# The gating products of four tokens in one turn of the generator, in a kernel of two transformer blocks

## The chip, the cores and the metric

The kernel runs on one core of one Trainium2 chip. The time is the device time of one execution in microseconds (us); lower is better. The engines of the core are TensorE (PE in the profile, its weight loads PEld), VectorE (DVE), ScalarE (ACT), GpSimd (POOL) and SyncE (SP), which here issues DMAs. Each runs its own instructions in order and waits for others by semaphores.

## The reference, cut to what matters

Two blocks are computed, one after the other, on 256 tokens of width 1024. The part that is changed lies in the first block, in a layer of experts that each head picks for each token. Of 16384 experts, numbered (i, j) with i and j from 0 to 127, each of 8 heads picks 16 per token and gives each a gate.

```python
def expert_block(args):
    ht, it, gt = args
    ue = jnp.take(u, it, axis=0)
    act = jax.nn.gelu(jnp.einsum('tkd,td->tk', ue, ht), approximate=False)
    ve = jnp.take(v, it, axis=0)
    return jnp.einsum('tk,tkd->td', gt * act, ve)
```

The kernel takes no rows out of u or v. It multiplies all of u with all tokens, applies the Gelu, and multiplies by a dense matrix of gates that is zero for experts not picked; then it multiplies all of v with the result.

## The kernel before, in words

The weights come in pieces of 128 x 1024, one piece for a slot. A piece is loaded by SyncE's queue (wraw, four buffers), cast by ScalarE to a high part (wh) and subtracted by VectorE to a low part (wl), and each product is made of three matmuls: hH with wh, hL with wh, hH with wl. In the part of u a slot makes one row j of 128 experts for all 256 tokens: 24 matmuls into a PSUM tile named v, 12 in each half of the slot. ScalarE then applies the Gelu and VectorE multiplies by the gates where they are known already. The rows are kept in bigA (72 rows) and bigB (56 rows).

The gates of a token are a 128 x 128 matrix, made on TensorE as a product of two one-hot matrices over the token's 128 picks: A (ohA) has the place of j, B (ohB) the place of i times the gate. `onehots(g)` makes those of a pair of tokens (NG is 2): VectorE makes A of both and B of the first; B of the second is made on ScalarE in two steps (Abs, then Relu) or on VectorE, as a model of the engines' clocks decides when the program is built. There are three buffers of such pairs. `gates_mm(g, pg)` multiplies a pair into half of a PSUM tile pg for four tokens, which is named mm or aux in turn. `gates_ev(g, pg)` takes four tokens out of PSUM: for rows that are made already (there are J of them) VectorE multiplies the gates into bigA and bigB; for the rows still to come ScalarE copies the gates there, and the row is multiplied when it is made (`ev_u`).

`g_gates` is a generator that does all of this between the u products. `slot` and `half` call `step()`, once after the first half of the products and once after the second, and each `step()` advances every generator by one turn, as long as the modelled clocks of VectorE and ScalarE aren't too far ahead of TensorE's. The cast wh for the slot after the next but one is issued behind the first `step()` of a slot, the subtraction wl for the next but one ahead of its second. The order that comes out is fixed when the program is built. All engine calls go through one helper, so the profile gives them line 217; they are told apart by their tiles.

At the start of the gating 44 rows of u are made, so 84 slots of u follow.

Of the kernel before, what the change touches and what calls it, by code (L numbers as in the profile page):

```python
# [22 lines left out]
F32 = mybir.dt.float32  # L23
# [8 lines left out]
T = 256  # L32
# [275 lines left out]
def build(tc, xT, memT, smalls, smalls2, w1, keysT, uT, vT, w2, outT, stop=None):  # L308
# [8 lines left out]
    ps = es.enter_context(tc.tile_pool(name="ps", bufs=2, space=PSUM))  # L317
# [919 lines left out]
    NK = NKEY  # L1237
# [65 lines left out]
    NG = 2  # L1303
# [147 lines left out]
    def onehots(g):  # L1451
        t = NG * g
        A, B = ohs[g % 3]
        V.tensor_tensor(A, iota[:, None, :].to_broadcast([128, NG, 128]),
                        idxT[0][:, t:t + NG, None].to_broadcast([128, NG, 128]), op=OP.is_equal)
        for q in range(NG):
            i2, gg = idxT[1][:, t + q:t + q + 1], idxT[2][:, t + q:t + q + 1]
            if q % 2 and clock.t["S"] < clock.t["V"] + 500:

                S.activation(B[:, q], iota, AF.Abs, scale=-1.0, bias=i2)  # L1460
                S.activation(B[:, q], B[:, q], AF.Relu, scale=ngT[:, t // 2:t // 2 + 1], bias=gg)
            else:
                V.tensor_scalar(B[:, q], iota, i2, gg, op0=OP.is_equal, op1=OP.mult)
        oh[g] = (A, B)

    def gates_mm(g, pg):
        A, B = oh.pop(g)
        for q in range(NG):
            PE.matmul(pg[:, g % 2 * NG + q], A[:, q], B[:, q], start=True, stop=True)

    def gates_ev(g, pg):
        J = st["j"]
        ts = slice(4 * g, 4 * g + 4)
        for b, j0, j1 in bigs:
            lo, hi = j0, min(j1, J)
            if hi > lo:
                view = b[:, lo - j0:hi - j0, ts].rearrange("p j t -> p t j")
                V.tensor_tensor(view, view, pg[:, :, lo:hi], op=OP.mult)
            lo = max(j0, J)
            if j1 > lo:  # L1480
                view = b[:, lo - j0:j1 - j0, ts].rearrange("p j t -> p t j")
                S.copy(view, pg[:, :, lo:j1])
        st["g"] = g + 1

    def g_gates():
        onehots(0)
        onehots(1)
        yield
        pend = None
        for k in range(T // NG):  # L1490
            if k % 2 == 0:
                pg = ps.tile([128, 4, NK], F32, name="mm" if k % 4 else "aux")
            gates_mm(k, pg)
            if k % 2 == 0 and pend is not None:
                gates_ev(*pend)
            if k + 2 < T // NG:
                onehots(k + 2)
            pend = (k // 2, pg)
            clock.at(0.0)
            yield  # L1500
        gates_ev(*pend)

    go(g_gates())
    lim[0] = 2 * LIMIT
    while nu < NK:
# [26 lines left out]
    k = 0  # L1532
# [876 lines left out]
```

## Time and profile before

| what | value |
| --- | --- |
| time, median of 3 runs | 1461.38 us (1456.76 to 1477.7) |
| the profiled execution's own time | 1469.8 us |
| its span, first to last instruction | 1468.1 us |
| TensorE busy, mean granted clock | 97% of the span, 0.991 |
| VectorE, ScalarE, GpSimd busy | 73%, 58%, 12% |
| the gating | from the first one-hot at 388.5 us to the last at 622.8 us |
| u slots without gating behind it | until 684 us |

Busy shares are those of the whole span. The stages differ much from this mean, so they are read by windows of their own. A matmul's duration in the trace is longer than the step from its start to the next one's, since matmuls overlap; the same holds, less so, for short instructions on ScalarE and VectorE.

### The profile page before, as it was taken

The page shows a single profiled execution, that of the slowest core. Times are in us where ns is not written, and L with a number is a line of the kernel's source. Part 1 is how long each engine was busy: PE and PEld are TensorE (multiplying, and loading weights), DVE is VectorE, ACT ScalarE, POOL GpSimd, SP SyncE. Part 2 cuts the span into 40 slices and gives each one's busy share as a digit, 9 for nine tenths or more (in the row PEclk, how much of TensorE's full clock was granted, in tenths as well). Part 3 has the DMA queues.
Part 4 walks back from the last instruction along what each step waited for, and adds up shares of the span by engine and source line. Part 5 has one row for each costly group of instructions (what it writes and reads, how often), then busy time and mean ns, then how long its engine had stood idle before and what let it go on. Part 6 is the DMA issues. An engine that isn't in the chain of part 4 may idle for free.

```text
span 1468.1 us, 30208 instructions
## 1 busy us (share of the span) xinstructions
PE 1426.5 (97%) x11904; PEld 1398.6 (95%) x11904; DVE 1075.8 (73%) x2096; ACT 850.1 (58%) x1617; POOL 181.2 (12%) x228
## 2 busy tenths in 40 slices
PE   8999999999999999999999999999999999999997
PEld 8799998999999999999999989999998899999996
DVE  7866679899888999955555557555699774786665
ACT  5753454445699998844444455454575554655553
POOL 6100032014300000000000030000025420410000
PEclk9999999999999999999999999999999999999998
DMA  6334553545544443454555565555532443455552
GB/s 216 130 115 144 174 200 132 198 162 176 172 143 144 143 143 144 145 186 173 186 185 187 202 219 190 199 188 200 171 127 80 159 170 114 172 189 188 186 187 72
DMA packets 66381, 242.64 MB, mean 165 GB/s; under 512 B 7488, under 2 KB 7488, under 8 KB 65856
## 3 DMA queue, kind: packets, MB, share of 16 engines
q1 hardware_dynamic: 65664, 237.01, 47.0%
q0 software_dynamic: 432, 3.69, 0.7%
q8 instruction: 93, 1.52, 0.4%
q14 instruction: 48, 0.39, 0.1%
q10 hardware_dynamic: 144, 0.03, 0.0%
HBM read 239.64 MB, written 1.05 MB: 164 GB/s over the span
## 4 chain that ended last, share of the span: by engine, by line
PE 83%; DVE 9%; POOL 3%; issue 2%; ACT 2%; DMA 1%; DVEq 0%; ACTq 0%; POOLq 0%
PE v L217 49%; PE mm L217 28%; PE aux L217 6%; DVE wl L217 2%; DVE yc L217 1%; DMA s2t<-smalls_dram 1%; DVE x L217 1%; POOL hL L217 1%; DVE eq L217 1%; DVE hL L217 0%; POOL eq L217 0%; DVE pos L217 0%; DVE nt L217 0%; DVE xa L217 0%; ACT wh L217 0%
## 5 line engine op out<-in xcount | busy, mean ns | idle before, releaser
L217 DVE TENSOR_TENSOR wl<-wraw,wh 128x1024 fp32r<-128x1024 f32 x444 | 556.0, 1255 | 56.9 <-issue 45.7
L217 ACT CAST wh<-wraw 128x1024 fp32r<-128x1024 f32 x444 | 463.9, 1045 | 227.4 <-issue 123.5
L217 PE MATMUL v<-hH,wh 128*128 128x256 f32 x2048 | 583.5, 285 | 1.4 <-ACT hH L217 1.4
L217 PE MATMUL v<-hH,wl 128*128 128x256 f32 x2048 | 571.6, 279 | 4.3 <-DVE wl L217 4.3
L217 PE MATMUL v<-hL,wh 128*128 128x256 f32 x2048 | 571.5, 279 | 2.1 <-POOL hL L217 2.0
L217 PEld LDWEIGHTS v<-hH,wl 128*128 128x128 f32 x2048 | 386.7, 189 | 6.3 <-DVE wl L217 6.3
L217 PEld LDWEIGHTS v<-hL,wh 128*128 128x128 f32 x2048 | 386.7, 189 | 3.3 <-POOL hL L217 3.1
L217 PEld LDWEIGHTS v<-hH,wh 128*128 128x128 f32 x2048 | 385.4, 188 | 1.9 <-ACT hH L217 1.9
L217 PE MATMUL mm<-hH,wh 128*128 128x256 f32 x656 | 190.7, 292 | 7.7 <-DVE au L217 3.9
L217 PE MATMUL mm<-hL,wh 128*128 128x256 f32 x656 | 184.0, 284 | 3.1 <-DVE hL L217 2.5
L217 PE MATMUL mm<-hH,wl 128*128 128x256 f32 x656 | 185.5, 284 | 1.1 <-DVE wl L217 1.1
L217 PEld LDWEIGHTS mm<-hH,wh 128*128 128x128 f32 x656 | 127.1, 194 | 12.5 <-ACT wh L217 4.7
L217 PEld LDWEIGHTS mm<-hL,wh 128*128 128x128 f32 x656 | 125.7, 193 | 4.2 <-DVE hL L217 3.1
L217 PEld LDWEIGHTS mm<-hH,wl 128*128 128x128 f32 x656 | 126.8, 193 | 1.7 <-DVE wl L217 1.6
L217 DVE TENSOR_TENSOR hL<-bigA,hH 128x256 fp32r<-128x256 f32 x72 | 31.7, 441 | 77.5 <-ACT hH L217 77.4
L217 PE MATMUL mm<-h5H,wh 128*128 128x256 f32 x272 | 76.4, 281 | 0.0
L217 PE MATMUL mm<-h5L,wh 128*128 128x256 f32 x272 | 76.4, 281 | 0.0
L217 PE MATMUL mm<-h5H,wl 128*128 128x256 f32 x272 | 76.4, 281 | 0.0
L217 DVE TENSOR_TENSOR hL<-bigB,hH 128x256 fp32r<-128x256 f32 x56 | 23.8, 426 | 68.3 <-ACT hH L217 68.3
L217 ACT ACTIVATE ohB<-ohB,gT,ngT 128x128 f32<-128x128 f32 x126 | 62.3, 494 | 4.2
L217 ACT ACTIVATE bigA<-v 128x256 f32<-128x256 f32 (+14 forms) x72 | 25.8, 358 | 67.1 <-PE v L217 67.1
L217 DVE TENSOR_TENSOR ohA<-iota,i1T 128x256 f32<-128x256 f32 x128 | 53.6, 419 | 13.5 <-PE aux L217 6.5
(548 smaller groups left out, 2402.6 us busy)
## 6 DMA issues: line engine op xcount, KB each, us to landing
wraw<-w_dram SPq DMA_DIRECT2D x192, 512.0 KB, 3.5
wraw<-uT_dram SPq DMA_DIRECT2D x128, 512.0 KB, 3.3
wraw<-vT_dram SPq DMA_DIRECT2D x128, 512.0 KB, 3.3
s2t<-smalls_dram POOLq DMA_DIRECT2D x1, 1552.0 KB, 13.4
x<-xT_dram SPq DMA_DIRECT2D x4, 256.0 KB, 5.6
kyT<-keysT_dram POOLq DMA_DIRECT2D x1, 1024.0 KB, 7.1
xm<-memT_dram POOLq DMA_DIRECT2D x1, 1024.0 KB, 8.8
outT_dram<-z SPq DMA_DIRECT2D x4, 256.0 KB, 2.8
```

Source lines behind the costliest of these rows:

```text
L217: r = f(out, *a, **k)
```

## The change

`g_gates` makes the one-hots of three pairs at its start instead of two, and in each turn it now multiplies two pairs (four tokens, one PSUM tile), takes the four tokens of the turn before out of PSUM, and makes the one-hots of the next two pairs. Before, a turn had one pair, and every second turn took four tokens out.

```diff
     def g_gates():
-        onehots(0)
-        onehots(1)
+        for g in range(3):
+            onehots(g)
         yield
         pend = None
-        for k in range(T // NG):
-            if k % 2 == 0:
-                pg = ps.tile([128, 4, NK], F32, name="mm" if k % 4 else "aux")
+        for k in range(0, T // NG, 2):
+            pg = ps.tile([128, 4, NK], F32, name="mm" if k % 4 else "aux")
             gates_mm(k, pg)
-            if k % 2 == 0 and pend is not None:
+            gates_mm(k + 1, pg)
+            if pend is not None:
                 gates_ev(*pend)
-            if k + 2 < T // NG:
-                onehots(k + 2)
+            for g in (k + 3, k + 4):
+                if g < T // NG:
+                    onehots(g)
             pend = (k // 2, pg)
             clock.at(0.0)
             yield
         gates_ev(*pend)
```

On TensorE, at the first gating products, before (the numbers behind ohA and ohB are those of the buffers):

```order
L217 MATMUL v<-hH,wl 128x256
L217 MATMUL aux<-ohB_4839,ohA_4838 128x128 x2
L217 MATMUL v<-hH,wh 128x256
L217 MATMUL v<-hL,wh 128x256
L217 MATMUL v<-hH,wl 128x256
```

And now, at the same place:

```order
L217 MATMUL v<-hH,wl 128x256
L217 MATMUL aux<-ohB_4839,ohA_4838 128x128 x2
L217 MATMUL aux<-ohB_4841,ohA_4840 128x128 x2
L217 MATMUL v<-hH,wh 128x256
L217 MATMUL v<-hL,wh 128x256
L217 MATMUL v<-hH,wl 128x256
```

Two pairs stand together. In both kernels 12 products into v lie between one such block and the next, all through the gating: there are 128 blocks of one pair before and 64 of two pairs now, so the last one comes after 32 slots instead of 64.

On ScalarE, one slot in the middle of the gating, before:

```order
L217 COPY bigA<-aux 128x4x14
L217 COPY bigB<-aux 128x4x56
L217 ACTIVATE ohB_4843<-iota,i2T 128x128
L217 ACTIVATE ohB_4843<-ohB_4843,gT,ngT 128x128
L217 ACTIVATE bigA<-v 128x196
L217 ACTIVATE v<-v 128x60
L217 ACTIVATE ohB_4839<-iota,i2T 128x128
L217 ACTIVATE ohB_4839<-ohB_4839,gT,ngT 128x128
L217 CAST wh<-wraw 128x1024
```

And now, from the cast of one slot to shortly before the next cast:

```order
L217 CAST wh<-wraw 128x1024
L217 COPY bigA<-mm 128x4x18
L217 COPY bigB<-mm 128x4x56
L217 ACTIVATE ohB_4843<-iota,i2T 128x128
L217 ACTIVATE ohB_4843<-ohB_4843,gT,ngT 128x128
L217 ACTIVATE ohB_4839<-iota,i2T 128x128
L217 ACTIVATE ohB_4839<-ohB_4839,gT,ngT 128x128
L217 ACTIVATE bigA<-v 128x168
L217 ACTIVATE v<-v 128x88
L217 COPY bigA<-aux 128x4x17
L217 COPY bigB<-aux 128x4x56
```

Behind these come two more one-hots, of two steps each, and then the next cast. A slot has two pairs of copies and four one-hots where it had one and two; the cast and the two Gelus stay single.

On VectorE, one slot in the middle of the gating, before:

```order
L217 TENSOR_TENSOR bigA<-bigA,aux 128x4x58
L217 TENSOR_TENSOR ohA_4842<-iota,i1T 128x256
L217 TENSOR_SCALAR ohB_4843<-iota,i2T,gT 128x128
L217 TENSOR_TENSOR bigA<-bigA,v 128x56
L217 TENSOR_TENSOR ohA_4838<-iota,i1T 128x256
L217 TENSOR_SCALAR ohB_4839<-iota,i2T,gT 128x128
L217 TENSOR_TENSOR wl<-wraw,wh 128x1024
```

And now:

```order
L217 TENSOR_TENSOR bigA<-bigA,v 128x56
L217 TENSOR_TENSOR bigA<-bigA,aux 128x4x52
L217 TENSOR_TENSOR ohA_4840<-iota,i1T 128x256
L217 TENSOR_SCALAR ohB_4841<-iota,i2T,gT 128x128
L217 TENSOR_TENSOR ohA_4842<-iota,i1T 128x256
L217 TENSOR_SCALAR ohB_4843<-iota,i2T,gT 128x128
L217 TENSOR_TENSOR wl<-wraw,wh 128x1024
L217 TENSOR_TENSOR bigA<-bigA,mm 128x4x52
L217 TENSOR_TENSOR ohA_4838<-iota,i1T 128x256
L217 TENSOR_SCALAR ohB_4839<-iota,i2T,gT 128x128
L217 TENSOR_TENSOR ohA_4840<-iota,i1T 128x256
L217 TENSOR_SCALAR ohB_4841<-iota,i2T,gT 128x128
```

The multiplies of the gates and the one-hots are doubled for each wl. In all, 126 one-hots B are made on ScalarE and 130 on VectorE in both kernels. Behind the gating the rows of every engine stand in the same order as before, up to the numbers of buffers.

## Rows read from the trace of the kernel before

**Rows 1.** The page's first part: busy us, share of the span, instructions.

```profile
PE 1426.5 (97%) x11904; PEld 1398.6 (95%) x11904; DVE 1075.8 (73%) x2096; ACT 850.1 (58%) x1617; POOL 181.2 (12%) x228
```

**Rows 2.** Windows: us, busy of PE, PEld, DVE, ACT, POOL; granted clock, DMA share, GB/s.

```profile
390.00:508.00 118.00, 118.00 (x1027) 118.00 (x1026) 103.48 (x226) 111.07 (x281) 0.00 (x0) 1.00 0.43 148
508.00:627.00 119.00, 119.00 (x1036) 119.00 (x1035) 116.76 (x254) 105.20 (x256) 0.00 (x0) 1.00 0.41 143
628.00:684.00 56.00, 56.00 (x478) 56.00 (x478) 31.59 (x42) 26.71 (x41) 0.00 (x0) 1.00 0.52 184
```

**Rows 3.** The chain that ended last, in order of time: start, us, engine, tile, count.

```profile
394.65 1.42 PE v L217 x12
398.34 1.42 PE v L217 x12
...
626.91 57.96 PE v L217 x492
```

**Rows 4.** Tile ohB on ScalarE: count, ns min/median/max, first and last start.

```profile
L217 ACT ACTIVATE ohB<-iota,i2T x126: 382/393/406, 390.8 to 622.3; 128x128 f32<-128x128 f32 x126
L217 ACT ACTIVATE ohB<-ohB,gT,ngT x126: 492/494/498, 391.3 to 622.8; 128x128 f32<-128x128 f32 x126
```

**Rows 5.** Timeline of ScalarE over one gated slot: start, us, operation.

```profile
447.12 0.26 ACT L217 COPY bigA<-aux 128x56 f32<-128x56 f32 x1
447.22 0.57 ACT L217 COPY bigB<-aux 128x224 f32<-128x224 f32 x1
447.58 0.39 ACT L217 ACTIVATE ohB<-iota,i2T 128x128 f32<-128x128 f32 x1
448.00 0.49 ACT L217 ACTIVATE ohB<-ohB,gT,ngT 128x128 f32<-128x128 f32 x1
448.40 0.32 ACT L217 ACTIVATE bigA<-v 128x196 f32<-128x196 f32 x1
448.75 0.20 ACT L217 ACTIVATE v<-v 128x60 f32<-128x60 f32 x1
448.87 0.40 ACT L217 ACTIVATE ohB<-iota,i2T 128x128 f32<-128x128 f32 x1
449.30 0.50 ACT L217 ACTIVATE ohB<-ohB,gT,ngT 128x128 f32<-128x128 f32 x1
449.70 1.04 ACT L217 CAST wh<-wraw 128x1024 fp32r<-128x1024 f32 x1
450.81 0.25 ACT L217 COPY bigA<-mm 128x52 f32<-128x52 f32 x1
```

**Rows 6.** Timeline of VectorE over the same slot; idle time before an instruction in brackets.

```profile
446.38 0.71 DVE L217 TENSOR_TENSOR bigA<-bigA,aux 128x232 f32<-128x232 f32 x1
447.00 0.42 DVE L217 TENSOR_TENSOR ohA<-iota,i1T 128x256 f32<-128x256 f32 x1
447.33 0.34 DVE L217 TENSOR_SCALAR ohB<-iota,i2T,gT 128x128 f32<-128x128 f32 x1
447.58 0.21 DVE L217 TENSOR_TENSOR bigA<-bigA,v 128x56 f32<-128x56 f32 x1
448.17 0.43 DVE L217 TENSOR_TENSOR ohA<-iota,i1T 128x256 f32<-128x256 f32 x1 [0.38 <-PE mm L217]
448.51 0.34 DVE L217 TENSOR_SCALAR ohB<-iota,i2T,gT 128x128 f32<-128x128 f32 x1
448.77 1.22 DVE L217 TENSOR_TENSOR wl<-wraw,wh 128x1024 fp32r<-128x1024 f32 x1
```

**Rows 7.** Waits between 388 and 628 us: waiting, releaser, us in total, times, longest.

```profile
ACT bigB L217 <- DVE bigB L217: 10.0, 33, 0.4
```

**Rows 8.** Windows, as rows 2, at three short stretches where TensorE idles.

```profile
854.00:856.00 2.00, 0.54 (x2) 0.34 (x3) 1.90 (x3) 2.00 (x4) 0.76 (x4) 1.00 0.02 6
...
1106.00:1108.00 2.00, 0.74 (x4) 0.77 (x5) 1.93 (x6) 1.81 (x5) 0.00 (x0) 0.86 0.55 207
1108.00:1110.00 2.00, 2.00 (x11) 2.00 (x11) 1.97 (x5) 1.98 (x4) 1.92 (x2) 0.50 0.14 55
```

## The prediction

> **What bounds the kernel now.** I read the page's list of engines first: TensorE is busy for 97% of the span and ScalarE for 58% [rows 1], so over the whole program a ScalarE instruction costs nothing. That average doesn't hold for the stage which is changed. The windows show the stage from 390 to 627 us as two halves [rows 2]: TensorE has no idle time in either, ScalarE is busy 111.07 of 118 us in the first and 105.20 of 119 in the second, VectorE 103.48 and 116.76. Three engines are within a few per cent of full there. From 628 to 684 us, when the gating is over and the same u slots go on, TensorE is still full but VectorE (31.59 of 56) and ScalarE (26.71) are half idle. Then the chain that ended last: during the gating it steps with a period of 398.34 - 394.65 = 3.69 us, one slot, and after it runs 492 u products in 57.96 us, that is 0.1178 us each and 24 x 0.1178 = 2.83 us for a slot without gating [rows 3]. So TensorE sets the pace now: 64 gated slots of 3.69 us (236.0 us), then 20 bare ones.
>
> **What a gating product costs TensorE.** A gated slot has the 24 u products and four gating products: (3.687 - 2.827) / 4 = 0.215 us each. The two blocks of two are already no dearer than four single products would be, if nothing else hides in that difference; there is no cost of changing over between the two kinds of product that fewer blocks could save. I take that gain as zero; it is bounded above by what the difference leaves unexplained, a few ns a block.
>
> **What the change does to the pace.** The generator of the gating is advanced twice in a slot, after each half. Before, one turn brings two tokens, so a slot brings four. Now one turn brings four tokens, and the turns are not fewer: the table of TensorE's order has a block of four gating matmuls behind every 12 u products, so eight tokens in each slot. The 256 tokens are done after 32 slots instead of 64; the description's "once per slot" is not what the order shows. The sum of the work is the same on TensorE; on ScalarE and VectorE it is nearly the same, but compressed into half as many slots. Everything behind the stage stands in the same order as before.
>
> **TensorE's own need.** 2.827 + 8 x 0.215 = 4.55 us for each of 32 gated slots, and 2.83 for each of the 32 slots set free. That makes 145.5 + 90.5 = 236.0 us, the old time: alone it would be no change.
>
> **ScalarE's need.** I take the instructions' starts rather than their durations, since one begins before the last has landed: the wide copy lasts 0.57 us but the next starts 0.36 after it. The slot in [rows 5] has mid-size copies (56 elements to bigA), like the middle of the new stage. From start to start: copy to bigA 0.10, copy to bigB 0.36, first step of a one-hot 0.42 and 0.43, second 0.40 and 0.40, the two Gelus 0.35 and 0.12, the cast wh 1.11, of which 1.03 to 1.04 is its duration and some 0.08 is a wait before the copy. The sum is 3.69: ScalarE fills the slot. With eight tokens the slot has one cast (1.03), one pair of Gelus (0.47), two pairs of copies (2 x 0.46 = 0.92) and four one-hots (4 x 0.825 = 3.30): **5.72 us**. The number of one-hots on ScalarE (126 pairs of steps) and on VectorE stays as it is [rows 4]. Copies are longer at the stage's start (112 elements to bigA) and the ones to bigA vanish in its last four slots, which moves the mean by less than 0.1; I hold 5.6 as the floor.
>
> **VectorE's need.** In the slot of [rows 6]: multiply of the gates 0.62, one-hot A 0.33, B 0.25, multiply of the row 0.21, and the weights' low part wl 1.22. Doubled where it doubles: 2 x 0.62 + 4 x 0.585 + 0.21 + 1.22 = 5.0 us. It is above TensorE's 4.55 as well, but below ScalarE's, so ScalarE comes last.
>
> **Where it lands.** TensorE can't run ahead. The one-hots of a turn's second pair are made in the turn before, the three buffers allow no more; and the cast wh of the weights three slots on stands in ScalarE's queue behind the same one-hots. So in the 32 gated slots TensorE goes at ScalarE's 5.72 us instead of its own 4.55. To this comes the one wait per slot that the row already shows before a copy, 0.08, since the copies still follow VectorE's multiply into the same buffer: 5.80. The stage is then 32 x 5.80 + 32 x 2.827 = 185.6 + 90.5 = 276.1 us against 236.0, **+40 us**. Nothing later gives this back: the rows after it are the same, with TensorE at 97% over the program [rows 1]. The DMA isn't in the way of the free slots: 184 GB/s was reached at that pace from 628 to 684 us [rows 2].
>
> The profiled execution took 1469.8 us (span 1468.1, 1.7 outside it), 8.4 us over the median of 1461.4. The sum is a difference made inside one profile; I add it to the median: 1461.4 + 40.1 = **1501 us**, 2.7% slower. 2% is 29 us, about what a measurement of this kernel can tell from no change.
>
> **Rivals.**
> *ScalarE keeps up* (not slower). If ScalarE, when pressed, could start its instructions closer together than in the rows, the stage would stay TensorE's. At 4.55 us a slot or less the time is 1461 us; at 5.46 (236.0 + 29.2 = 32 x 5.46 + 90.5) the loss reaches 2%. For it: ScalarE was never pressed harder than 94%. Against it: the first step of a one-hot lasts 382 to 406 ns in all 126 cases [rows 4], the second reads its result and can't start sooner, and these steps are 3.3 of the 5.7 us. 18% for everything under 5.46, 4% of it for the full 4.55.
>
> *The two engines wait for each other.* ScalarE waited 33 times for VectorE's multiply into bigB, 10.0 us together, 0.3 us each, in the stretch where VectorE was nearly full [rows 7]. There is one such copy in a slot there; now there are two, on a VectorE that is 5.0/5.7 full. If both wait 0.3 the slot is 6.32, the stage 202.2 + 90.5 = 292.7 and the time 1518 us. Against it: in the slot of [rows 5, 6] the copy starts as the multiply ends (446.38 + 0.71 against 447.12) and loses only the 0.08 us, and VectorE's need of 5.0 us in 5.7 leaves it 0.7 a slot to get ahead. 14%.
>
> *TensorE's clock falls.* With 4.55 us of work in 5.8, TensorE will stand idle for a fifth of the stage in gaps of about 0.6 us. The rows show what a fall takes here: after TensorE was busy for only 0.74 of 2 us at 1106 the granted clock was 0.86, then 0.50 (1.2 of the 2.4 GHz) in the next 2 us; but at 854 us, with 0.54 of 2 us busy, it stayed at 1.00 [rows 8]. At the lower level a gated slot would need 9.1 us; over half of the 32 slots that is 16 x 9.1 + 16 x 5.8 + 90.5 = 328.9, so 1554 us. The gaps that I expect are far shorter than either of these stretches, hence 4%.
> The Trainium skill's page "TensorE: Matmul & The Clock Gate", section "A second HAM failure mode: psum-queue depth-cycling", has a rule that speaks against the change: many short idles between groups of matmuls can make the clock swing between its two levels. By that rule the time would be this rival's; the trace has no stage of that pattern, so no row decides it.
>
> *The change is once per slot after all* (64 slots of 3.69, 1461 us) has no chance, since the order is fixed when the program is built.
>
> **How the numbers follow.** The forecast, ScalarE bound with 5.46 to 6.1 us a slot, has 64%; under 5.46 is 18%, the lockstep 14%, the clock 4%. The range leaves out the clock, the full gain of the first rival and half of what lies near 1461: from 5.36 us a slot (+26, 1488) to 6.4 (+59, 1520). All cases but the first rival are slower by over 2%: 0.82. Of its 18%, 0.17 is within 2% and 0.01 faster by over 2%, since no part of the change takes work from TensorE.
>
> **What would show it.** Right: gated blocks of eight matmul records per half slot, a gated stage of about 185 us with a period near 5.8, TensorE near 80% busy with its waits put down to ScalarE's ohB, ScalarE without idle time, and then 52 bare slots at 2.83. Wrong: a period near 4.6 (ScalarE can go faster), waits of ScalarE for bigA or bigB of half a us in each half slot (lockstep), a granted clock under 0.95 in the stage, or a free stretch slower than 2.83 us a slot.

## The result and the profile after

The changed kernel takes 1505.3 us (median of four runs, 1500.6 to 1509.7) against 1462.3 for the kernel before (also four runs): a ratio of 1.026, 95% interval 1.022 to 1.030. It is slower, by 43 us where 40 were forecast. The profiled execution took 1509.0 us, with a span of 1507.3.

The windows of the kernel after, over the two halves of its gating and over the same stretch without gating as in [rows 2] (columns as there):

```profile
390.00:480.00 90.00, 78.67 (x605) 71.61 (x604) 69.26 (x174) 80.01 (x213) 0.00 (x0) 1.00 0.27 90
480.00:578.00 98.00, 87.95 (x644) 77.93 (x642) 83.11 (x195) 87.78 (x238) 0.00 (x0) 1.00 0.25 88
628.00:684.00 56.00, 56.00 (x497) 56.00 (x496) 31.59 (x42) 26.74 (x42) 0.00 (x0) 1.00 0.56 191
```

Before, TensorE had no idle time here; now it has 11.3 of 90 us and 10.0 of 98. No engine is full: ScalarE is busy for 89 and 90%, VectorE for 77 and 85%. The clock is 1.00 throughout. The waits between 388 and 585 us, longest first (waiting, releaser, us in total, times, longest):

```profile
DVE bigA L217 <- ACT bigA L217: 34.8, 29, 1.8
PEld mm L217 <- ACT ohB L217: 18.2, 31, 0.8
PEld aux L217 <- ACT ohB L217: 14.6, 28, 0.6
ACT bigA L217 <- DVE bigA L217: 13.5, 28, 0.6
PE mm L217 <- ACT ohB L217: 12.3, 31, 0.6
PE aux L217 <- ACT ohB L217: 9.2, 28, 0.4
```

TensorE waits for ScalarE's one-hots, about once a turn. ScalarE waits for VectorE's multiply 28 times, once a slot, and VectorE for ScalarE 29 times. What that is can be seen in one slot on ScalarE:

```profile
470.34 0.27 ACT L217 COPY bigA<-aux 128x64 f32<-128x64 f32 x1 [0.47 <-DVE bigA L217]
470.45 0.55 ACT L217 COPY bigB<-aux 128x224 f32<-128x224 f32 x1
...
472.44 1.04 ACT L217 CAST wh<-wraw 128x1024 fp32r<-128x1024 f32 x1
473.39 0.26 ACT L217 COPY bigA<-mm 128x64 f32<-128x64 f32 x1
...
475.48 0.28 ACT L217 ACTIVATE bigA<-v 128x152 f32<-128x152 f32 x1
475.79 0.24 ACT L217 ACTIVATE v<-v 128x104 f32<-128x104 f32 x1
476.51 0.27 ACT L217 COPY bigA<-aux 128x60 f32<-128x60 f32 x1 [0.48 <-DVE bigA L217]
```

and on VectorE and TensorE at the same place:

```profile
474.30 0.26 DVE L217 TENSOR_TENSOR bigA<-bigA,v 128x96 f32<-128x96 f32 x1
475.79 0.69 DVE L217 TENSOR_TENSOR bigA<-bigA,aux 128x228 f32<-128x228 f32 x1 [1.23 <-ACT bigA L217]
```

```profile
473.51 0.83 PE L217 MATMUL mm<-ohB,ohA 128*128 128x128 f32 x6
474.81 0.49 PE L217 MATMUL mm<-ohB,ohA 128*128 128x128 f32 x2 [0.46 <-ACT ohB L217]
```

The slot lasts from 470.34 to 476.51, 6.17 us, in which ScalarE stands idle for 0.48. The wait is a hand-over. The last thing that ScalarE does in a slot is the Gelu of the newest row (475.48, done at 475.76). VectorE's multiply of the gates covers the rows up to that one, so it can't start before 475.79. ScalarE's copy into the same buffer follows that multiply (done at 476.48), at 476.51. Without the wait it would have started sooner than the end of the second Gelu: in the slot of [rows 5] and with the copies first (below) the next instruction starts 0.12 to 0.16 us after that Gelu's start, here 0.72. By starts, then, the wait costs this slot some 0.6 us and ScalarE's work takes 5.6. In the slot of [rows 5] the Gelu stood 2.4 us ahead of the copies (448.40 against 450.81), with a one-hot and the cast between, so the chain was hidden.

The first multiply into bigA out of an aux tile starts at 395.0 and the last of 32 at 583.6; two neighbours are a slot apart, so the mean gated slot is 188.6 / 31 = 6.08 us, against (623.4 - 394.8) / 62 = 3.69 before, where two slots lie between them. Two rows of the chain of work that ended last, the bare slots of u and a stretch of v behind them (start, us in the step, engine, tile, line, count):

```profile
584.62 138.72 PE v L217 x1224
728.21 143.41 PE v L217 x1261
```

1224 products in 138.72 us, 2.72 us a slot where [rows 3] has 2.83. The first cast of the part of v, where u is done, starts at 727.8 us against 685.2 before, 42.6 us later. The spans of the two profiles differ by 39.2 us (1507.3 against 1468.1), so all of the loss is made in the changed stage, and behind it the new profile is 3.4 us the quicker one.

### The profile page after: what moved, and what is told of

The parts are those of the page before. It is cut to its first block, busy times and chain, and to the rows that moved or that the text cites. A ratio compares the mean times of both kernels' runs of the same rounds, so it can differ in the third digit from the quotient of the medians.

```text
span 1507.3 us, 30270 instructions
## 1 busy us (share of the span) xinstructions
PE 1444.6 (96%) x11904; PEld 1398.5 (93%) x11904; DVE 1064.9 (71%) x2067; ACT 852.4 (57%) x1613; POOL 182.1 (12%) x228
## 3 DMA queue, kind: packets, MB, share of 16 engines
q0 software_dynamic: 432, 3.69, 0.7%
HBM read 239.64 MB, written 1.05 MB: 160 GB/s over the span
## 4 chain that ended last, share of the span: by engine, by line
PE 69%; DVE 12%; ACT 12%; issue 3%; POOL 2%; DMA 1%; DVEq 0%; ACTq 0%; POOLq 0%; SPq 0%
PE v L217 40%; PE mm L217 25%; ACT ohB L217 6%; PE aux L217 4%; DVE wl L217 3%; ACT wh L217 2%; DVE bigA L217 2%; ACT bigB L217 2%; ACT bigA L217 1%; DVE yc L217 1%; DMA wraw<-vT_dram 1%; DVE x L217 1%; POOL hL L217 1%; DVE eq L217 0%; DVE tmp L217 0%
## 5 line engine op out<-in xcount | busy, mean ns | idle before, releaser
L217 PE MATMUL v<-hH,wh 128*128 128x256 f32 x2048 | 574.1, 280 | 1.2 <-ACT hH L217 1.2
L217 ACT ACTIVATE v<-v 128x256 f32<-128x256 f32 (+16 forms) x84 | 27.7, 330 | 72.5 <-PE v L217 71.5
```

The lines of the kernel that those rows point to most:

```text
L217: r = f(out, *a, **k)
```

## The experiments

Theory: with eight tokens a slot, ScalarE's work (5.7 us a slot) and a hand-over of 0.5 us set the pace. Rivals: the block of four or its early one-hots cost by themselves, or, in a later run, any turn that follows another at half a slot does (A); a chain between the engines, not the sum of work, sets the pace (B); only ScalarE was in the way of TensorE's 4.55 us (C); the wait is there in any order (D). In each run's profile the mean gated slot is worked out from the multiplies into bigA as above. Each ratio is to runs of the kernel before that were taken beside it, with medians of 1462.3 to 1465.1 us; slots and "u done at" are from one profile of each kernel.

| kernel | tokens a slot | gated slot, us | u done at, us | time, us | ratio to before |
| --- | --- | --- | --- | --- | --- |
| before | 4 | 3.69 | 685.2 | 1462.3 | |
| after | 8 | 6.08 | 727.8 | 1505.3 | 1.026 (1.022 to 1.030) |
| once per slot | 4 | 3.67 | 684.8 | 1460.5 | 0.999 (0.995 to 1.003) |
| two turns in three | 5.33 | 4.33 | 702.0 | 1479.2 | 1.007 (1.003 to 1.011) |
| two turns in five | 3.2 | 3.50 | 684.6 | 1463.8 | 0.9995 (0.997 to 1.002) |
| no Relu step (work left out) | 8 | 5.03 | 700.6 | 1476.5, one run | |
| second one-hot on GpSimd | 8 | 4.94 | 695.5 | 1473.0, one run | |
| all one-hots on VectorE | 8 | 5.87 | 721.9 | 1496.4, one run | |
| copies first | 8 | 5.58 | 716.8 | 1495.4 | 1.023 (1.018 to 1.028) |
| gates out last, shares held | 8 | 5.57 | 720.7 | 1501.2 | 1.022 (1.014 to 1.030) |
| gates out last, shares free | 8 | 5.05 | 695.7 | 1478.6 | 1.010 (1.005 to 1.016) |
| before, copies first | 4 | 3.68 | 683.9 | 1467.0 | 1.001 (0.998 to 1.004) |

**Once per slot.** An empty turn behind each full one:

```diff
             pend = (k // 2, pg)
-            clock.at(0.0)
-            yield
+            for _ in range(2):
+                clock.at(0.0)
+                yield
```

> The changed kernel, but with an empty turn of the generator behind each full one: four tokens come together still, and only once per slot. Theory (ScalarE's work per slot is the bound in the changed kernel, 5.7 us and a wait of 0.5 us): ScalarE's need is again about 3.7 us a slot and TensorE's 3.69, so the gating takes 64 slots of 3.7 us and the time is that of the kernel before, 1455 to 1470 us, ratio 0.995 to 1.01. Rival A (a block of four gating products, or their one-hots made a turn ahead, is dear in itself): the time stays near the changed kernel's, over 1490 us.

Measured 1460.5 us and 3.67 us a slot, the kernel before in all but the grouping; TensorE is busy for 40.00 of 40 us in every window of 40 us of the stage. Rival A falls: four tokens in one block, with their one-hots made a turn ahead, cost nothing and win nothing. What does harm is that a full turn follows at every half slot, which doubles the rate.

**Two turns in three, two in five.** The same edit with `1 + (k // 2) % 2` and `2 + (k // 2) % 2` turns.

> The changed kernel with one empty turn behind every second full one: 5.33 tokens a slot, 48 gated slots. ScalarE's need per slot is 1.50 + 1.333 x 2.11 = 4.3 us, TensorE's 3.97. Theory (loss = slots x what the fullest engine needs over TensorE): 48 x (4.3 to 4.6) + 36 x 2.83 against 64 x 3.69 + 20 x 2.83, that is 16 to 30 us over the kernel before, 1478 to 1492 us. Rival A (any turn that is made a half slot after another costs the same, here 32 such pairs of turns): half of the changed kernel's loss, also about 1483, but in slots that alternate. Rival E (up to some rate nothing is lost): 1462 us.

> The other way: two full turns in five, 3.2 tokens a slot, 80 gated slots of the 84. ScalarE's need is 3.2 us a slot and VectorE's 2.7 to 3.3, TensorE's 2.83 + 3.2 x 0.215 = 3.52. Theory (TensorE sets the pace at any rate up to four tokens a slot, and its sum is the same): the time of the kernel before, 1455 to 1470 us, ratio 0.99 to 1.01. If a slower rate still won something (ScalarE or VectorE cost TensorE time in the kernel before too), it would be under 1450 us.

At 5.33 tokens a slot the mean gated slot is 4.33 us and u is done 16.8 us later than before. The time, 1479, is in the range, though the ratio (1.003 to 1.011, some 5 to 16 us) puts the loss at or below the lower end of what was forecast. The slot comes out near ScalarE's mean need of 4.3 us, but ScalarE isn't full: between 400 and 560 us it is busy for 35.78 to 38.19 us of each 40 (the model of the clocks gave it 120 one-hots here, not 126).

```profile
440.00:480.00 40.00, 38.23 (x321) 36.94 (x319) 35.34 (x86) 35.78 (x97) 0.00 (x0) 1.00 0.36 126
...
520.00:560.00 40.00, 38.76 (x328) 37.81 (x328) 39.64 (x96) 38.19 (x93) 0.00 (x0) 1.00 0.38 131
```

Between 395 and 575 us it waits 19 times for a multiply into bigA, 10.0 us together, and TensorE's own waits for ScalarE's one-hots stand at one tile alone:

```profile
ACT bigA L217 <- DVE bigA L217: 10.0, 19, 0.6
PE mm L217 <- ACT ohB L217: 6.2, 21, 0.5
```

That tile, mm, belongs to the second of two full turns that lie half a slot apart. So the loss does alternate, as this form of rival A has it, and the mean need hides that. Its size is smaller than the rival's: half of the changed kernel's loss, with the bare slots at the pace that they had before, is (42.6 + 5.6) / 2 = 24 us at the end of u, against 16.8. The once-per-slot run has no such pair of turns and says nothing on it. At 3.2 tokens the slot is 3.50 us, TensorE's 3.52, and the time does not move. So at 3.2 and at four tokens a slot TensorE sets the pace and its sum is the same; at 5.33 and at eight time is lost.

**No Relu step; GpSimd; VectorE alone.** Three kernels take one-hots, or in the first their second step, away from ScalarE.

```diff
                 S.activation(B[:, q], iota, AF.Abs, scale=-1.0, bias=i2)
-                S.activation(B[:, q], B[:, q], AF.Relu, scale=ngT[:, t // 2:t // 2 + 1], bias=gg)
```

```diff
-            if q % 2 and clock.t["S"] < clock.t["V"] + 500:
+            if False:
...
-                V.tensor_scalar(B[:, q], iota, i2, gg, op0=OP.is_equal, op1=OP.mult)
+                (G if q % 2 else V).tensor_scalar(B[:, q], iota, i2, gg, op0=OP.is_equal, op1=OP.mult)
```

In the third kernel only the first of the last two edits is made.

> The changed kernel without the second step (Relu) of the one-hots that ScalarE makes, so the gates of every second token are wrong. Takes 4 x 0.40 us a slot from ScalarE: its need falls from 5.7 to 4.1 us and VectorE's 5.05 comes last. Theory (the fullest engine sets the pace): gated slot from 6.1 to 5.0 to 5.3 us, time 1471 to 1482 us. Rival B (the wait of ScalarE's copy for VectorE's multiply, and of that for the Gelu, is what sets the pace, a chain and not the sum of the work): the slot falls by less than 0.5 us, time over 1488 us. Rival C (TensorE would reach its own 4.55 us): under 1463 us.

> The changed kernel with the second one-hot of each pair made on GpSimd, in one step, instead of on ScalarE; nothing is left out. ScalarE's need falls to 2.4 us a slot, VectorE's stays at 5.05. Theory: the pace is VectorE's, or GpSimd's if one such one-hot lasts over 1.2 us: gated slot 5.0 to 5.3 us, time 1471 to 1482 us, and still slower than before, since VectorE too has more work than TensorE at eight tokens a slot. Rival C (only ScalarE was in the way): the slot falls to TensorE's 4.55 us, time 1457 us. If GpSimd and VectorE disturb each other the slot stays over 5.5 us.

> The changed kernel with every one-hot on VectorE; nothing is left out. ScalarE's need falls to 2.4 us a slot, VectorE's rises by four instructions of 0.255 us to 6.05. Theory (the fullest engine sets the pace, whichever it is): gated slot 6.0 to 6.3 us, 32 of them, time 1498 to 1512 us, as in the changed kernel, now with VectorE full and ScalarE waiting. Rival B (the chain through ScalarE's two-step one-hots sets the pace): the slot falls to 5 us, time under 1480 us.

Windows of 40 us in the middle of the gating, in this order:

```profile
480.00:520.00 40.00, 38.63 (x319) 37.10 (x318) 40.00 (x95) 28.30 (x87) 0.00 (x0) 1.00 0.32 102
```

```profile
480.00:520.00 40.00, 38.67 (x321) 37.21 (x320) 40.00 (x96) 20.12 (x56) 40.00 (x33) 1.00 0.32 104
```

```profile
480.00:520.00 40.00, 34.51 (x271) 32.44 (x272) 40.00 (x111) 17.41 (x49) 0.00 (x0) 1.00 0.28 93
```

The fifth column, VectorE, is full in all three, and the slots are close to VectorE's needs: 5.03 and 4.94 us where 5.05 was worked out, and 5.87 for 6.05, so that the last two fell a little below the expected ranges (5.0 and 6.0 upwards). Taking 1.6 us a slot from ScalarE brought 1.05, down to the next engine and not to TensorE's 4.55: rival C falls. With the two-step chain gone altogether the all-VectorE kernel is nearly as slow as the changed one: a loss of this size does not need rival B's chain, only a full engine. The time of that run is 1.6 us below its range. On GpSimd a one-hot took 776 to 2771 ns, median 1288, beside a full VectorE; GpSimd too is busy without a gap, so that kernel may have two bounds.

**Copies first.** The hand-over alone is taken away, by issuing ScalarE's copies ahead of the multiplies in `gates_ev`:

```diff
         for b, j0, j1 in bigs:
-            lo, hi = j0, min(j1, J)
-            if hi > lo:
-                view = b[:, lo - j0:hi - j0, ts].rearrange("p j t -> p t j")
-                V.tensor_tensor(view, view, pg[:, :, lo:hi], op=OP.mult)
             lo = max(j0, J)
             if j1 > lo:
                 view = b[:, lo - j0:j1 - j0, ts].rearrange("p j t -> p t j")
                 S.copy(view, pg[:, :, lo:j1])
+        for b, j0, j1 in bigs:
+            lo, hi = j0, min(j1, J)
+            if hi > lo:
+                view = b[:, lo - j0:hi - j0, ts].rearrange("p j t -> p t j")
+                V.tensor_tensor(view, view, pg[:, :, lo:hi], op=OP.mult)
```

> The changed kernel with ScalarE's copies of the gates issued ahead of VectorE's multiplies, so that they no longer wait for these; the multiplies now wait for the copies. Nothing is left out. Theory (the sum of ScalarE's work, and 0.5 us of hand-over on top): the 0.5 us a slot goes, the gated slot is 5.6 to 5.75 us instead of 6.1, and the time is 10 to 15 us under the changed kernel, 1488 to 1496 us, still slower than before by 2%. Rival B (the hand-over makes the loss): near 1465 us. Rival D (the wait only moves to VectorE's one-hots, which now come late for TensorE): no change, 1500 to 1510 us.

> The kernel before, with the copies of the gates issued ahead of the multiplies, as in the experiment on the changed kernel. Theory (ScalarE's wait for the multiply costs only where ScalarE sets the pace): no change, 1455 to 1470 us, ratio 0.995 to 1.005. If the hand-over costs TensorE time here too: 3 to 10 us less.

The gated slot falls by 0.50 us and u is done 11.0 us sooner than in the changed kernel: 32 x 0.50 = 16 us, less the 5.6 us by which the bare slots were slower in this profile (last section). The medians differ by 10 us, but the intervals of the two ratios overlap, so it is the slots that show it. Rival B, that the hand-over makes the loss, fails: the slot is still 1.0 us above TensorE's 4.55. The copy now starts behind the Gelu without a wait, and ScalarE is nearly full:

```profile
473.55 0.25 ACT L217 ACTIVATE v<-v 128x112 f32<-128x112 f32 x1
473.71 0.26 ACT L217 COPY bigA<-aux 128x56 f32<-128x56 f32 x1
```

```profile
480.00:520.00 40.00, 36.71 (x291) 34.09 (x290) 36.96 (x87) 38.78 (x109) 0.00 (x0) 1.00 0.28 94
```

The waits between 395 and 575 us name another releaser for TensorE:

```profile
PEld mm L217 <- DVE ohB L217: 20.8, 31, 0.8
```

These waits are put down to VectorE's one-hots, which now stand behind a multiply that comes later; rival D is right that a wait shows up there, but the slot is shorter all the same. In the kernel before, the same edit changes nothing, since TensorE is the bound there.

**Gates out last.** `gates_ev` moves to the end of a turn, behind the one-hots, which parts the Gelu and the copies without changing the order of multiply and copy.

```diff
-            if pend is not None:
-                gates_ev(*pend)
             for g in (k + 3, k + 4):
                 if g < T // NG:
                     onehots(g)
+            if pend is not None:
+                gates_ev(*pend)
```

The clock model then gives ScalarE 102 one-hots instead of 126; in the first kernel the share is held by `if q % 2 and g > 1:`.

> The changed kernel with the gates taken out of PSUM at the end of a turn, behind the one-hots, instead of ahead of them; the shares of ScalarE and VectorE in the one-hots are held at 126 and 130. VectorE's multiply still comes ahead of ScalarE's copies, but the Gelu of the newest row then lies four ScalarE instructions back. Theory (the multiply waits for that Gelu, and the copy for the multiply): the hand-over of 0.5 us a slot goes, gated slot 5.6 to 5.8 us instead of 6.1, 1488 to 1496 us, as with the copies first. Rival D (any order has the hand-over, since both engines write one buffer): 1500 to 1510 us.

> The same with the shares left to the model of the clocks, which now gives ScalarE 102 of the 256 one-hots B and VectorE 154. ScalarE's need is 1.50 + 0.92 + 3.19 x 0.825 = 5.05 us a slot, VectorE's 5.05 + 0.81 x 0.255 = 5.26. Theory (the fullest engine sets the pace): gated slot 5.2 to 5.6 us, 1474 to 1487 us: the smallest loss at eight tokens a slot that these two engines allow, still slower than before. Rival (the pace is ScalarE's chain of one-hots as such): as the run beside it, over 1488 us.

With the shares held the gated slot is 5.57 us and ScalarE 97% busy, as with the copies first, and between 395 and 575 us no wait of ScalarE for a multiply into bigA is left. So the hand-over needs two things: the copy behind the multiply, and the newest row's Gelu right ahead of both. Taking away either one, as these two experiments do, is enough. The time, 1501 us from four runs between 1487 and 1505, is above the expected range and inside rival D's; it does not settle it, and the slots and the missing waits do. With free shares, ScalarE (38.83 of 40 us) and VectorE (40.00) are both full, or nearly so, between 440 and 480 us, and the slot is 5.05 us, below the expected 5.2: VectorE's need was put 0.2 us too high here as in the all-VectorE kernel. The time is 1478.6, still 1.0% slower than before; at eight tokens a slot only the GpSimd kernel, timed once, did the whole work in less (1473.0). Nothing beat the kernel before, and the two-in-five run says why: it already runs at TensorE's sum.

## Why the prediction was right

- **TensorE sets the pace before, and neither grouping nor a lower rate wins anything.** Shown: 0.999 once per slot, 0.9995 at two turns in five.
- **The change doubles the rate.** Shown by the last gating multiply at 585.5 us instead of 627.0, after 32 slots, and by the run that halves the rate again.
- **ScalarE's need is the bound, and 5.72 us was 0.14 too much for it.** The slots are 5.58 and 5.57 where no hand-over was left and ScalarE was 97% busy. The cast was put at 1.03, its duration, but without a wait the next instruction starts 0.95 us after the cast's start (472.44 and 473.39 above); the old slot's 1.11 thus held a wait of 0.16, not 0.08. The first Gelu's step is 0.31, not 0.35 (475.48 and 475.79). VectorE's 5.0 came out at 5.03 when ScalarE was relieved.
- **The wait of 0.08 us a slot is the mis-sized term.** It was taken over from the old slot; it is 6.08 - 5.58 = 0.50. The lockstep rival had the right pair, ScalarE's copy behind VectorE's multiply, but the wrong reason (a full VectorE) and count (two waits a slot): VectorE was not full, it waited 1.2 us itself, for the Gelu that had moved next to it. The mean slot was 6.08 instead of 5.80, 32 x 0.28 = 9.0 us more: 13.4 for the wait, less 4.5 for ScalarE's need.
- **The bare slots were sized at 2.83 and took 2.72 us** in this profile, 52 x 0.107 = 5.6 us less. That is one of two paces of TensorE (below), and no run shows that the change brings it. 40.1 + 9.0 - 5.6 = 43.5 us, against 42.6 measured at the end of u. That the forecast came so close is in part luck: three errors, of which two offset the third. The 0.215 us of a gating product rests on the slower pace for all 24 products of a slot; half of them ran at the faster one (below), so it is nearer to 0.23. Nothing hangs on it here, since TensorE wasn't the bound.
- **The clock stayed at 1.00** over the gating, though TensorE stopped some 59 times for up to 0.6 us. The Trainium skill's page "TensorE: Matmul & The Clock Gate" (section "A second HAM failure mode: psum-queue depth-cycling") tells of a kernel whose short idles between groups of matmuls made the clock swing between its levels; gaps of this kind did not do so in any profile here.
- **Starts, not durations, were the measure to sum.** A one-hot's second step lasts 0.49 us and the next instruction starts 0.40 after it. The Trainium skill's page "ScalarE: Activation LUTs", section "What ACT_TABLE_LOAD costs", says that ACTIVATEs in a row overlap by about 93 ns; the traces agree there, but not behind a one-hot's first step, whose result the next one reads (0.39 us long, 0.42 or 0.43 to the next start), nor behind the first of the two Gelus (0.32 long and 0.35 to the next start in [rows 5]), where no run shows why. The sum of such steps over a slot is the length of the slot, whichever engine sets the pace, so the prediction's 3.69 does not show that ScalarE filled it; its need is that sum less the waits within it.

## What to carry to other kernels

When side work is packed into fewer slots, compare the need per slot of every engine, not the total: an engine at 58% of the span set the pace here because it was at 94% in the one stage that was compressed. Take the steps from start to start over one slot of the old trace, less the waits that they hold, double what doubles, and see which engine comes last. Then look which instructions have become neighbours on each queue: a chain over two engines that was hidden behind a cast can surface as a wait that no row of the old trace shows.

## What was not expected of the hardware

TensorE's products of 256 columns run at two paces, at the same granted clock of 1.00: 0.1178 to 0.1182 us or 0.1133 to 0.1138 (this one in both rows of the chain above: 138.72 / 1224 and 143.41 / 1261). The kernel before has both: 0.1178 over the 492 products of [rows 3], and 0.1133 here:

```profile
877.65 168.66 PE v L217 x1488
```

In a stream of these products alone one pace holds over hundreds of them. It changes behind a stop of TensorE, and also without a stop, behind a block of gating products: in the kernel before the pace alternates from half slot to half slot all through the gating (start, us, engine, line, operation).

```profile
446.34 0.28 PE L217 MATMUL v<-hH,wl 128*128 128x256 f32 x1
...
447.40 0.28 PE L217 MATMUL v<-hH,wl 128*128 128x256 f32 x1
447.52 0.61 PE L217 MATMUL mm<-ohB,ohA 128*128 128x128 f32 x4
447.89 0.37 PE L217 MATMUL v<-hH,wh 128*128 128x256 f32 x1
...
448.56 0.28 PE L217 MATMUL v<-hH,wl 128*128 128x256 f32 x1
...
449.24 0.28 PE L217 MATMUL v<-hH,wl 128*128 128x256 f32 x1
```

The nine steps to 447.40 are 1.06 / 9 = 0.1178 us each, the six to 449.24 are 0.68 / 6 = 0.1133, and no row has idle time before it. The bare u slots ran at the faster pace in the changed kernel, the all-VectorE kernel and the gates-out-last kernel with free shares, and at the slower one in all other runs; the 1488 products of v shown above took the slower one in only two (the kernel before with the copies first, and gates out last with free shares: 175.25 us instead of 168.66). It follows neither the edit nor the engines' load in any way that these runs show, and what sets it stays open. It is worth 4% of such a stretch, 5.6 us in 52 slots of u, so single times here differ by more than some of the effects, and the slots in the profile decide where the medians don't.
